# Seven of the twelve column blocks of mod[2] to mod[4]: products on ScalarE and sums on GpSimd, in a diffusion trunk with a mixture of experts

## The chip, the cores and the metric

The kernel runs on one core of a Trainium2 chip. The metric is device time in microseconds (us), the median of several runs. The core's engines are called here by the profile's names: PE (TensorE, matmuls), DVE (VectorE), ACT (ScalarE), POOL (GpSimd), SP (the queue that issues the large transfers).

## The reference

One layer (DEPTH is 1, so mixer 0, the gated convolution, and no context stream). 256 tokens, width 2048, float32, 16 experts.

```python
mod = split(silu(c) @ mod_w + mod_b, 6)                 # six rows of 2048
h   = x * (1 + mod[1]) + mod[0]
gate_b, gate_c, val = split(h @ conv_in_w, 3)           # 2048 -> 3 x 2048
o   = (gate_b * depthwise_conv3(gate_c * val)) @ conv_out_w
x   = layer_norm(ALPHA * x + mod[2] * o)
h2  = x * (1 + mod[4]) + mod[3]
x   = layer_norm(ALPHA * x + mod[5] * hier_moe(h2))     # top-1 group, top-2 of its 4 experts
```

The change concerns mod[2], mod[3] and mod[4]: each is a product of one vector of 2048 with a matrix of 2048 x 2048 from HBM (16 MB each).

## The kernel before

All weights stream through a ring of six SBUF tiles of 128x3072 (`RING`). `get(i)` issues the loads on SP in the order of the list of steps, as far ahead as places in the ring come free; a load waits on its place's last reader.

The product for mod is done in blocks of 512 columns. A block is three ring tiles: 6, 6 and 4 slices of 128x512, one for each of the 16 k tiles `kt`; the vector silu(c) is `sT`, one column for each k tile. A block is made in one of two ways. On TensorE (`gemv_rows` for mod[2] and mod[5], `gemv_cols` for the others): 16 matmuls with `sT` as the stationary operand into a PSUM tile `gv`, line 273 or 300. On VectorE (`gemv_cols` with `on_vector`, chosen by `ON_V`): ScalarE writes the first product into a tile `rows` (line 275), VectorE adds the other 15 (line 278), two at each split (`VN`). For mod[2] the four partial rows of `gv` are added and broadcast to all partitions by a matmul with a selector, `gb` (line 313), and copied into `mod2b` (line 314). For mod[3] and mod[4] the block is transposed, `gc` (line 250), and reduced.

The input projection `conv_in_w` runs in steps (`cin_step`). A step takes a tile with three parts (gate_b, gate_c, val). For each part `split` has ScalarE cast it to a rounded hi (line 395, names `hic`), VectorE subtract for lo (line 396, `loc`), and TensorE run 24 matmuls of 256 columns (lines 403 to 405) with the two halves of h. hi and lo have two buffers each (`whi`, `wlo`). In a full step's names, `hic8_22` is the hi of the step that begins at k tile 8, column group 2, part 2.

The first four column groups are done in five passes over k (`KGS`: 2, 2, 4, 4 and 4 k tiles), called pass 0 to 4 here, since h becomes known block by block from mod[0] and mod[1]; each pass adds into `acc` (line 464). The blocks of mod[0] and mod[1] of the next pass, and so many tiles of mod[2] to mod[4] as `EXTRA` says, are merged among the pass's first three steps. Then come the other four column groups, four steps each, and the output projection `conv_out_w` (`cout_step`, two splits of 1024 columns each, names `hio`), which multiplies by `mod2b` (line 565) and, for its second and third quarter, has GpSimd add the result to x (line 569). The rest of the tiles of mod[2] to mod[4] is merged among these, one for each step. `router_prep` then needs mod[3] and mod[4]. The experts' weights follow, 302 MB.

The program's order on each engine is not the order of the code alone: the scheduler places instructions of one engine by when it expects their operands. What order came out is shown below, with the change.

Of the kernel before, what the change touches and what calls it, by code (L numbers as in the profile page):

```python
# [9 lines left out]
F32 = mybir.dt.float32  # L10
# [9 lines left out]
P = 128  # L20
# [10 lines left out]
ACC_GROUPS = 4  # L31
YB = 4
DRIP = (1, 6, 3)
EXTRA = [0, 1, 0, 0, 12]
KGS = [2, 2, 4, 4, 4]
BEFORE = 4
EARLY = 3
VN = 2
AT = 1
ON_V = [[0, 1, 0, 1], [0, 1, 1, 1]]  # L40
CG = 8

CAPS = [32, 128, 128, 128, 64, 64, 64] + [32] * 9
# [23 lines left out]
def trunk_kernel(  # L67
# [33 lines left out]
    def aux_tile(name):  # L101
        return psum.tile([P, 512], F32, tag="aux", bufs=2, name=name)
# [125 lines left out]
                      start=True, stop=True)  # L228


    pending, queue = [], []

    def mod_load(m, c0, n, t0, nt):
        def load(w):
# [3 lines left out]
            )  # L238
        return load

    def gemv_cols(m, c0, n, on_vector=False):


        box = {}
        nb, k0 = n // P, c0 // P

        def late():
            pt = aux_tile(f"gc{m}_{c0}")
            for i in range(nb):
                TE.transpose(pt[:, i * P : (i + 1) * P], box["r"][:, i * P : (i + 1) * P], ident)  # L250
            sm = const.tile([P, 4], F32, tag="gsum", bufs=2, name=f"gs{m}_{c0}")
            V.tensor_reduce(out=sm[:, :nb], in_=pt[:, :n].rearrange("p (i c) -> p i c", i=nb)[:, :, :: 1 if on_vector else 32],
                            axis=AX.X, op=ALU.add)
            V.scalar_tensor_tensor(
                out=modT[:, m, k0 : k0 + nb], in0=sm[:, :nb], scalar=1.0 if m in (1, 4) else 0.0,
                in1=modbT[:, m * KT + k0 : m * KT + k0 + nb], op0=ALU.add, op1=ALU.add)

        per = min(KT, 3072 // n)
        for t0 in range(0, KT, per):
            nt = min(per, KT - t0)  # L260

            def work(w, t0=t0, nt=nt):
                if t0 == 0:
                    if on_vector:
                        box["r"] = p1.tile([P, 512], F32, tag="rows", bufs=2, name=f"rows{m}{c0}")
                    else:
                        box["ps"] = aux_tile(f"gv{m}_{c0}")
                for k in range(nt):
                    kt = t0 + k
                    g = kt % 4  # L270
                    ws = w[:, k * n : (k + 1) * n]
                    if not on_vector:
                        TE.matmul(box["ps"][32 * g : 32 * g + 32, :n], sT[:, kt : kt + 1].to_broadcast([P, 32]), ws, start=kt < 4, stop=kt >= 12)  # L273
                    elif kt == 0:
                        S.mul(box["r"][:, :n], ws, sT[:, kt : kt + 1])
                    else:
                        def fn(ws=ws, kt=kt):
                            V.scalar_tensor_tensor(out=box["r"][:, :n], in0=ws, scalar=sT[:, kt : kt + 1],  # L278
                                                   in1=box["r"][:, :n], op0=ALU.mult, op1=ALU.add)
                            if kt == KT - 1:  # L280
                                pending.append(late)
                        queue.append(fn)
                if t0 + nt == KT and not on_vector:
                    box["r"] = p1.tile([P, 512], F32, tag="rows", bufs=2, name=f"rows{m}{c0}")
                    S.copy(box["r"][:, :n], box["ps"][:, :n])
                    pending.append(late)

            yield mod_load(m, c0, n, t0, nt), work

    def gemv_rows(m, q, dst, tile_fn, done):  # L290

# [22 lines left out]
        S.copy(dst, ps[:, :])  # L314


    bias_rows = {}
    for m, pool in ((2, p1), (5, const)):
        bias_rows[m] = pool.tile([P, 512], F32, name=f"bias{m}")
        G.memset(bias_rows[m], 0.0)  # L320
        S.dma_start(bias_rows[m][0:128:32, :], mod_b[0, m * D : (m + 1) * D].rearrange("(q c) -> q c", c=512))
# [25 lines left out]
    S.dma_start(rtw[:, :, 0:4], rt_grp_w[0].rearrange("(t p) c -> p t c", p=P))  # L347
    S.dma_start(rtw[:, :, 4:20], rt_exp_w[0].rearrange("(t p) c -> p t c", p=P))

    ii = p1.tile([P, P], I32, tag="rows", bufs=2, name="ii_128")  # L350
    G.iota(ii, pattern=[[1, P]], base=1, channel_multiplier=0)
    iota = const.tile([P, P], F32, name="iota")
    V.tensor_copy(iota, ii)
    ii = p1.tile([P, NOV], I32, tag="rows", bufs=2, name="ii_ov")
    G.iota(ii, pattern=[[1, NOV]], base=1, channel_multiplier=0)
    io32 = const.tile([P, NOV], F32, name="io32")
    V.tensor_copy(io32, ii)
# [34 lines left out]
    def split(src, n, name):  # L392
        hi = p1.tile([P, 1024], F32R, tag="whi", bufs=2, name=f"hi{name}")
        lo = p1.tile([P, 1024], F32R, tag="wlo", bufs=2, name=f"lo{name}")
        S.copy(hi[:, :n], src)  # L395
        V.tensor_sub(lo[:, :n], src, hi[:, :n].bitcast(F32))  # L396
        for fn in queue[:VN]:
            fn()
        del queue[:VN]
        return hi, lo  # L400

    def mm3(ps, whi, wlo, ahi, alo, start, stop):
# [49 lines left out]
        yhi[g], ylo[g] = yh, yl  # L452

    accs = [big_tile(f"acc{g}").rearrange("p (a t) -> p a t", a=3) for g in range(ACC_GROUPS)]
    mod2b = p1.tile([P, D], F32, name="mod2b")
    stats = const.tile([P, 2, 4, 6], F32, name="stats")

    def acc_step(i, g, hook=None):
# [19 lines left out]

    rp = {}

    def router_prep():
        flush()
        V.tensor_mul(G4, T2t[:, 0:16], modT[:, 4, :])
        V.tensor_mul(B3, T2t[:, 32:48], modT[:, 4, :])
        V.tensor_add(B3, B3, modT[:, 3, :])
        t3 = p1.tile([P, KT, 32], F32, tag="rows", bufs=2, name="rtB")
        sums = const.tile([P, 40], F32, name="rsums")
        V.tensor_tensor(out=t3, in0=rtw, in1=B3[:, :, None].to_broadcast([P, KT, 32]), op=ALU.mult)
        V.tensor_reduce(out=sums[:, 0:20], in_=t3[:, :, 0:20].rearrange("p k c -> p c k"), axis=AX.X, op=ALU.add)
        V.tensor_tensor(out=rtw, in0=rtw, in1=G4[:, :, None].to_broadcast([P, KT, 32]), op=ALU.mult)  # L490
        V.tensor_reduce(out=sums[:, 20:40], in_=rtw[:, :, 0:20].rearrange("p k c -> p c k"), axis=AX.X, op=ALU.add)

        def late():
            ps = aux_tile("rsum")
            TE.matmul(ps[:, 0:40], onesF.to_broadcast([P, P]), sums, start=True, stop=True)
            V.tensor_add(rb, rb, ps[:, 0:20])
            V.tensor_copy(rsum, ps[:, 20:40])

            pt = aux_tile("gbT")
            TE.transpose(pt[:KT, 0:P], G4, ident)  # L500
            TE.transpose(pt[:KT, P : 2 * P], B3, ident)
# [13 lines left out]
            V.tensor_copy(GB.rearrange("p s (q j) -> p s q j", j=4), ps[:, 0:32].rearrange("p (s j q) -> p s q j", s=2, j=4))
        pending.append(late)
# [799 lines left out]
```

## Time and profile before

| | us |
|---|---|
| median of 3 runs (1299.0 to 1299.91) | 1299.4 |
| the profiled execution, device time | 1300.78 |
| its span in the trace | 1299.1 |
| mean granted TensorE clock, share of full | 0.958 |

The profile is of one execution. Its page gives each engine's busy time; the trace behind it can be asked for stretches, for the instructions of one engine in time order, and for groups of like instructions. Matmuls are pipelined, so groups of different lines overlap, and a group's busy time is the union of its own spans.

### The profile page before, as it was taken

What the parts mean: (1) busy time and instruction counts of PE and PEld (TensorE: products, weight loads), DVE (VectorE), ACT (ScalarE), POOL (GpSimd) and SP (SyncE); (2) the same over time, 40 slices, a digit from 0 to 9 for tenths busy, and PEclk for the clock granted to TensorE, in tenths of its full rate; (3) what the DMA queues carried; (4) which work ended last, traced back from release to release, by engine and by line L of the source; (5) the groups of instructions that cost most, each with busy time, mean ns of one, the idle gap of its engine ahead of it and who ended that gap; (6) DMA issues with size and microseconds to landing.
All of it is one profiled execution on the core that took longest, in us unless ns stands there. A gap on an engine that the chain in (4) does not pass through costs nothing. (4 is left out here: it accounts for less than half of the span.)

```text
span 1299.1 us, 19675 instructions
## 1 busy us (share of the span) xinstructions
PE 1148.7 (88%) x7871; PEld 755.3 (58%) x7871; DVE 669.4 (52%) x1257; ACT 364.7 (28%) x634; POOL 36.2 (3%) x66
## 2 busy tenths in 40 slices
PE   4999999999999999887789997999689997789982
PEld 2778886878699965543257543674157443444352
DVE  1664555687879978442255642573146431123226
ACT  1332333433344424240035312451026110100020
POOL 1000000000300030000000000000000000000000
PEclk7999999999999999698899999999899999899996
DMA  9999889899999878899998899999999899999991
GB/s 310 372 388 396 301 286 399 305 315 338 348 316 347 306 270 282 366 412 430 429 409 349 321 422 428 405 360 376 428 430 425 338 429 429 429 428 430 429 396 69
DMA packets 151105, 475.61 MB, mean 366 GB/s; under 512 B 11000, under 2 KB 70104, under 8 KB 126688
## 3 DMA queue, kind: packets, MB, share of 16 engines
q1 hardware_dynamic: 145984, 471.89, 92.4%
q10 hardware_dynamic: 5024, 2.40, 0.6%
q8 instruction: 64, 1.05, 0.3%
q14 instruction: 33, 0.27, 0.1%
HBM read 472.16 MB, written 2.10 MB: 365 GB/s over the span
## 5 line engine op out<-in xcount | busy, mean ns | idle before, releaser
L986 PE MATMUL gue<-w,xgp 128*32 128x384 f32 (+1 forms) x1664 | 219.1, 538 | 63.6 <-DMA w<-in_ex_w_up_dram 55.7
L403 PE MATMUL ci<-hhi,hic 128*128 128x256 f32 x768 | 219.6, 287 | 2.3 <-ACT hic L395 1.4
L405 PE MATMUL ci<-hhi,loc 128*128 128x256 f32 x768 | 217.3, 284 | 3.8 <-DVE loc L396 3.6
L404 PE MATMUL ci<-hlo,hic 128*128 128x256 f32 x768 | 216.9, 283 | 0.6 <-DVE hlo L390 0.4
L986 PEld LDWEIGHTS gue<-w,xgp 128*32 128x32 f32 (+1 forms) x1664 | 81.3, 123 | 198.3 <-issue 90.1
L403 PEld LDWEIGHTS ci<-hhi,hic 128*128 128x128 f32 x768 | 145.4, 190 | 14.6 <-issue 8.4
L395 ACT CAST hic<-w 128x1024 fp32r<-128x1024 f32 (+1 forms) x108 | 102.5, 953 | 178.8 <-PE ci L404 153.3
L405 PEld LDWEIGHTS ci<-hhi,loc 128*128 128x128 f32 x768 | 145.1, 189 | 9.4 <-DVE loc L396 6.6
L404 PEld LDWEIGHTS ci<-hlo,hic 128*128 128x128 f32 x768 | 145.5, 189 | 5.4 <-DVE hlo L390 2.3
L396 DVE TENSOR_TENSOR loc<-w,hic 128x1024 fp32r<-128x1024 f32 (+1 forms) x108 | 118.5, 1106 | 34.2 <-ACT hic L395 32.0
L733 DVE TENSOR_TENSOR parts<-w,parts 128x384 fp32r<-128x384 f32 (+1 forms) x168 | 97.8, 612 | 56.8 <-ACT parts L732 55.5
L732 ACT CAST parts<-w 128x384 fp32r<-128x384 f32 (+1 forms) x168 | 89.7, 559 | 79.2 <-PE gue L983 59.5
L1005 ACT COPY gse<-gue 128x384 f32<-128x384 f32 x16 | 7.7, 481 | 313.9 <-PE gue L986 313.9
L858 PEld LDWEIGHTS gap<-ohp,xt 128*128 128x128 f32 x512 | 66.0, 209 | 22.6 <-issue 16.0
L858 PE MATMUL gap<-ohp,xt 128*128 128x128 f32 (+2 forms) x512 | 70.2, 294 | 5.0 <-DVE xgp L826 5.0
L986 PE MATMUL gue<-w,xfp 128*128 128x384 f32 x192 | 71.5, 495 | 1.7 <-DMA w<-in_ex_w_gate_dram 1.7
L273 PE MATMUL gv<-w,sT 128*32 128x512 f32 (+1 forms) x416 | 57.1, 567 | 7.5 <-DMA w<-in_mod_w_dram 7.5
L464 DVE TENSOR_TENSOR acc<-acc,ci 128x512 f32<-128x512 f32 x48 | 32.9, 686 | 58.8 <-PE ci L405 58.6
L1092 DVE TENSOR_TENSOR Y<-dne,m 32x512 f32<-32x512 f32 (+3 forms) x84 | 40.7, 484 | 37.4 <-PE dne L944 34.1
L278 DVE SCALAR_TENSOR_TENSOR rows<-w,sT,rows 128x512 f32<-128x512 f32 x75 | 57.8, 771 | 1.3
L558 PE MATMUL co<-loo,yh 128*128 128x512 f32 x128 | 51.5, 402 | 3.0 <-DVE loo L396 3.0
L826 DVE TENSOR_SCALAR xgp<-gap,GB 128x32 f32<-128x32 f32 (+1 forms) x104 | 31.5, 314 | 43.6 <-ACT xgp L824 43.1
(311 smaller groups left out, 1452.7 us busy)
## 6 DMA issues: line engine op xcount, KB each, us to landing
w<-in_ex_w_gate_dram SPq DMA_DIRECT2D x64, 1536.0 KB, 14.7
w<-in_ex_w_up_dram SPq DMA_DIRECT2D x64, 1536.0 KB, 16.8
w<-in_ex_w_down_dram SPq DMA_DIRECT2D x60, 1536.0 KB, 14.0
w<-in_mod_w_dram SPq DMA_DIRECT2D x48, 1536.0 KB, 8.9
w<-in_conv_in_w_dram SPq DMA_DIRECT2D x84, 512.0 KB, 6.9
w<-in_mod_w_dram SPq DMA_DIRECT2D x22, 1024.0 KB, 8.2
w<-in_conv_out_w_dram SPq DMA_DIRECT2D x16, 1024.0 KB, 6.6
w<-in_conv_in_w_dram SPq DMA_DIRECT2D x24, 256.0 KB, 6.3
```

The costliest lines, as they stand in the source:

```text
L273: TE.matmul(box["ps"][32 * g : 32 * g + 32, :n], sT[:, kt : kt + 1].to_broadcast([P, 32]), ws, start=kt < 4, stop=kt >= 12)
L278: V.scalar_tensor_tensor(out=box["r"][:, :n], in0=ws, scalar=sT[:, kt : kt + 1], in1=box["r"][:, :n], op0=ALU.mult, op1=ALU.add)
L395: S.copy(hi[:, :n], src)
L396: V.tensor_sub(lo[:, :n], src, hi[:, :n].bitcast(F32))
L403: TE.matmul(ps, whi, ahi, start=start, stop=False)
L404: TE.matmul(ps, whi, alo, start=False, stop=False)
L405: TE.matmul(ps, wlo, ahi, start=False, stop=stop)
L558: TE.matmul(pso[h][:, :], yh[:, k, a:b], wl, start=False, stop=False)
L732: S.copy(hi[:, :n], src)
L733: V.tensor_sub(lo[:, :n], src, hi[:, :n].bitcast(F32))
L858: TE.matmul(ps[:, k * n : (k + 1) * n], xn[:, h, (k0 + k) * P : (k0 + k + 1) * P], oh[:, h, :n], start=h == 0, stop=h == 1)
L986: TE.matmul(dst, big[0][:, KF.index(kt), :] if cc == 128 else xg[:, kt, :cc], src, start=st_, stop=sp_)
```

## The change

- mod[2] no longer uses TensorE for its products. `gemv_all` has ScalarE multiply each slice in place in its ring tile (`S.mul(ws, ws, ...)`) and GpSimd add it to the block's columns of `mod2b`, 64 products in all. `mod2b` starts as zeros with the bias in its first partition, so that the sum over partitions, still a matmul and a copy for each block (`finish`, tiles `gb`), includes the bias.
- Of mod[3] and mod[4], three blocks (`SHARED`) are made in the same way into a tile `rows`, the other five by VectorE. None is left to TensorE. Before, five were VectorE's and three TensorE's.
- The products wait in a list `shared`; each split issues one or two of them. `flush_shared` issues what is left ahead of the first step of the output projection, and in `router_prep`.
- `EXTRA` loads four of these tiles in each of passes 2, 3 and 4, in place of one in pass 1 and twelve in pass 4.
- `rows` has three buffers, one more than before; the memset of `mod2b` and the load of its bias stand at the program's start.

```diff
-EXTRA = [0, 1, 0, 0, 12]
+EXTRA = [0, 0, 4, 4, 4]
...
-ON_V = [[0, 1, 0, 1], [0, 1, 1, 1]]
+
+SHARED = [[0, 1, 0, 1], [0, 1, 0, 0]]
...
-    pending, queue = [], []
+    pending, queue, shared = [], [], []
+
+    def add_product(r, ws, kt, then):
+
+        def fn():
+            S.mul(ws, ws, sT[:, kt : kt + 1])
+            G.tensor_tensor(out=r(), in0=r(), in1=ws, op=ALU.add)
+            if kt == KT - 1:
+                then()
+        shared.append(fn)
...
-    def gemv_cols(m, c0, n, on_vector=False):
+    def gemv_cols(m, c0, n, how="PE"):
...
+        def row_tile():
+            box["r"] = p1.tile([P, 512], F32, tag="rows", bufs=3, name=f"rows{m}{c0}")
+
...
                     elif kt == 0:
-                        S.mul(box["r"][:, :n], ws, sT[:, kt : kt + 1])
+                        def fn(ws=ws):
+                            row_tile()
+                            S.mul(box["r"][:, :n], ws, sT[:, 0:1])
+                        (shared if how == "shared" else queue).append(fn)
+                    elif how == "shared":
+                        add_product(lambda: box["r"][:, :n], ws, kt, lambda: pending.append(late))
                     else:
...
+    def gemv_all(m, q, dst):
+
+        def finish():
+            ps = aux_tile(f"gb{m}{q}")
+            TE.matmul(ps[:, :], onesF.to_broadcast([P, P]), dst, start=True, stop=True)
+            S.copy(dst, ps[:, :])
+
+        for t0, nt in ((0, 6), (6, 6), (12, 4)):
+            def work(w, t0=t0, nt=nt):
+                for k in range(nt):
+                    add_product(lambda: dst, w[:, k * 512 : (k + 1) * 512], t0 + k, lambda: pending.append(finish))
+
+            yield mod_load(m, q * 512, 512, t0, nt), work
...
+    mod2b = p1.tile([P, D], F32, name="mod2b")
+    G.memset(mod2b, 0.0)
+    S.dma_start(mod2b[0:1, :], mod_b[0:1, 2 * D : 3 * D])
     bias_rows = {}
-    for m, pool in ((2, p1), (5, const)):
+    for m, pool in ((5, const),):
...
-        for fn in queue[:VN]:
-            fn()
-        del queue[:VN]
+        for todo_, n in ((queue, VN), (shared, 2 if len(shared) > 4 else 1)):
+            for fn in todo_[:n]:
+                fn()
+            del todo_[:n]
         return hi, lo
...
+    def flush_shared():
+        while shared:
+            shared.pop(0)()
+        old = pending[:]
+        pending.clear()
+        for fn in old:
+            fn()
+
     def router_prep():
+        flush_shared()
         flush()
...
         if m == 2:
-            o = mod2b[:, q * 512 : (q + 1) * 512]
-            return list(gemv_rows(m, q, o, aux_tile, lambda: pending.append(lambda: finish_rows(m, q, o))))
-        return list(gemv_cols(m, q * 512, 512, ON_V[m - 3][q]))
+            return list(gemv_all(m, q, mod2b[:, q * 512 : (q + 1) * 512]))
+        return list(gemv_cols(m, q * 512, 512, "shared" if SHARED[m - 3][q] else "DVE"))
...
-            rest += fs[:2] + qt + fs[2:]
+            rest += fs[:2] + ([(None, lambda w: flush_shared())] if g == ACC_GROUPS else []) + qt + fs[2:]
```

The order on the engines moves most in passes 2 and 3. ScalarE, from the cast of pass 3's third step on, before (w39 and w42 are projection tiles, gv0_1536 a block of mod[0]):

```order
L395 CAST hic8_21_1647<-w39_1474 128x1024
L285 COPY rows01536_1593<-gv0_1536_1478 128x512
L395 CAST hic8_22_1675<-w39_1474 128x1024
L395 CAST hic8_30_1727<-w42_1585 128x1024
L395 CAST hic8_31_1755<-w42_1585 128x1024
L285 COPY rows11536_1720<-gv1_1536_1599 128x512
L395 CAST hic8_32_1817<-w42_1585 128x1024
L387 ACTIVATE hhi_183<-xT120_1767,modT_105 128x256 x2
L395 CAST hic12_00_1855<-w43_1595 128x1024
L387 ACTIVATE hhi_183<-xT121_1780,modT_105 128x256 x2
```

Casts follow each other there, with one copy between. The same place now (w45 to w48 are tiles of mod[2], w49 the projection tile of the fourth step):

```order
L427 CAST hic8_22_1730<-w44_1513 128x1024
L419 ACTIVATE hhi_183<-xT121_1843,modT_105 128x256
L237 ACTIVATE w45_1523<-w45_1523,sT_94 128x512 x6
L237 ACTIVATE w46_1635<-w46_1635,sT_94 128x512 x4
L237 ACTIVATE w47_1647<-w47_1647,sT_94 128x512 x3
L310 COPY mod2b_108<-gb21_2035 128x512
L237 ACTIVATE w47_1647<-w47_1647,sT_94 128x512 x3
L237 ACTIVATE w48_1655<-w48_1655,sT_94 128x512 x3
L427 CAST hic8_30_1790<-w49_1663 128x1024
L237 ACTIVATE w48_1655<-w48_1655,sT_94 128x512
L427 CAST hic8_31_1822<-w49_1663 128x1024
```

Nineteen products and a copy of a broadcast now stand between the casts hic8_22 and hic8_30. In pass 2 it is the same with w31 to w34, 6, 6, 4 and 3 products ahead of hic4_30, without a copy among them.

TensorE, where block 1 of mod[2] is broadcast, before (in pass 4, behind six of its products):

```order
L300 MATMUL gv21_1974<-w46_1714,sT_94 32x512 x6
L313 MATMUL gb20_1981<-mod2b_189,selG_79 128x512
L300 MATMUL gv21_1974<-w47_1722,sT_94 32x512 x6
L403 MATMUL ci12_10_1996<-hhi_183,hic12_10_1999 128x256
L404 MATMUL ci12_10_1996<-hlo_184,hic12_10_1999 128x256
L405 MATMUL ci12_10_1996<-hhi_183,loc12_10_2000 128x256
```

It stood between products of the next block. Now, at the end of pass 3's third step:

```order
L436 MATMUL ci8_22_1669<-hhi_183,hic8_22_1730 128x256
L437 MATMUL ci8_22_1669<-hlo_184,hic8_22_1730 128x256
L438 MATMUL ci8_22_1669<-hhi_183,loc8_22_1731 128x256
L309 MATMUL gb21_2035<-mod2b_108,onesF_85 128x512
L436 MATMUL ci8_30_1787<-hhi_183,hic8_30_1790 128x256
L437 MATMUL ci8_30_1787<-hlo_184,hic8_30_1790 128x256
L438 MATMUL ci8_30_1787<-hhi_183,loc8_30_1791 128x256
```

The broadcast moved from the middle of pass 4 to between two steps of pass 3. It reads the sums of w34, w45 and w46. GpSimd had none of them before; its queue now holds there:

```order
L238 TENSOR_TENSOR mod2b_108<-mod2b_108,w45_1523 128x512 x6
L238 TENSOR_TENSOR mod2b_108<-mod2b_108,w46_1635 128x512 x4
L238 TENSOR_TENSOR mod2b_108<-mod2b_108,w47_1647 128x512 x6
L238 TENSOR_TENSOR mod2b_108<-mod2b_108,w48_1655 128x512 x6
```

These 22 sums, in this order, are new. Behind 241 us of the trace, at the second quarter of the output projection (rows31536 is a block of mod[3], xt the residual):

```order
L238 TENSOR_TENSOR rows31536_3268<-rows31536_3268,w77_2938 128x512 x5
L238 TENSOR_TENSOR rows31536_3268<-rows31536_3268,w79_3063 128x512 x5
L610 TENSOR_TENSOR xt_87<-xt_87,t100_3302 128x512
L610 TENSOR_TENSOR xt_87<-xt_87,t101_3305 128x512
L238 TENSOR_TENSOR rows31536_3268<-rows31536_3268,w79_3063 128x512
L238 TENSOR_TENSOR rows31536_3268<-rows31536_3268,w81_3160 128x512 x4
```

Two residual sums stand among the sums of the block.

## Rows read from the trace of the kernel before

**Rows 1.** The page's first part: engine, busy us (share of the span), instructions.
```profile
PE 1148.7 (88%) x7871; PEld 755.3 (58%) x7871; DVE 669.4 (52%) x1257; ACT 364.7 (28%) x634; POOL 36.2 (3%) x66
```

**Rows 2.** Stretches: us, engines' busy us (instructions), TensorE clock, DMA share, GB/s.
```profile
132.00:179.00 47.00, 46.73 (x371) 38.22 (x369) 26.59 (x38) 16.09 (x19) 0.00 (x0) 1.00 0.88 318
179.00:241.00 62.00, 57.56 (x432) 40.79 (x432) 38.72 (x55) 22.27 (x32) 0.00 (x0) 1.00 0.95 349
241.00:447.00 206.00, 202.48 (x1479) 179.80 (x1478) 167.22 (x208) 80.20 (x90) 13.54 (x8) 1.00 0.90 319
...
551.00:1285.00 734.00, 631.82 (x4220) 350.04 (x4212) 289.30 (x653) 171.58 (x389) 3.61 (x2) 0.96 0.95 395
```

**Rows 3.** ScalarE in time order: start, us, line, out<-in, [idle before, releaser].
```profile
119.18 1.05 ACT L395 CAST hic<-w 128x1024 fp32r<-128x1024 f32 x1 [1.76 <-PE ci L404]
122.00 1.05 ACT L395 CAST hic<-w 128x1024 fp32r<-128x1024 f32 x1 [1.77 <-PE ci L404]
...
178.82 1.05 ACT L395 CAST hic<-w 128x1024 fp32r<-128x1024 f32 x1 [0.43 <-PE ci L404]
...
240.53 1.05 ACT L395 CAST hic<-w 128x1024 fp32r<-128x1024 f32 x1 [1.80 <-PE ci L404]
243.38 1.05 ACT L395 CAST hic<-w 128x1024 fp32r<-128x1024 f32 x1 [1.80 <-PE ci L404]
```

**Rows 4.** TensorE groups, 178 to 244 us (two rows), then 244 to 447 us.
```profile
L300 PE MATMUL gv<-w,sT 128*32 128x512 f32 x116 | 15.8, 597 | 0.0
L313 PE MATMUL gb<-mod2b,selG 128*128 128x512 f32 x8 | 4.5, 644 | 2.8 <-DVE mod2b L305 2.8
...
L273 PE MATMUL gv<-w,sT 128*32 128x512 f32 x84 | 13.8, 602 | 0.0
```

**Rows 5.** ScalarE: line 275 (ns min/median/max), line 441 as a group, two in a row.
```profile
L275 ACT ACTIVATE rows<-w,sT x5: 717/727/727, 269.6 to 421.8; 128x512 f32<-128x512 f32 x5
...
L441 ACT ACTIVATE v<-u,T2t 128x256 f32<-128x256 f32 x16 | 7.3, 502 | 6.7 <-DVE u L436 6.7
...
447.84 0.91 ACT L441 ACTIVATE v<-u,T2t 128x256 f32<-128x256 f32 x2
```

**Rows 6.** GpSimd's sums (ns min/median/max), and VectorE's subtractions near one, in time order.
```profile
L569 POOL TENSOR_TENSOR xt<-xt,t x16: 1274/1452/2289, 334.9 to 479.1; 128x512 f32<-128x512 f32 x16
...
354.44 1.22 DVE L396 TENSOR_TENSOR loc<-w,hic 128x1024 fp32r<-128x1024 f32 x1 [3.36 <-ACT hic L395]
...
357.15 1.55 DVE L396 TENSOR_TENSOR loc<-w,hic 128x1024 fp32r<-128x1024 f32 x1 [0.29 <-ACT hic L395]
```

**Rows 7.** DMA issues by form: count, KB each, median us from issue to landing.
```profile
w<-in_conv_in_w_dram SPq DMA_DIRECT2D x84, 512.0 KB, 6.9
```

**Rows 8.** Three stretches of 4 us about an idle, and TensorE's first matmul behind it.
```profile
664.00:668.00 4.00, 2.36 (x10) 1.06 (x6) 3.97 (x19) 0.26 (x1) 0.00 (x0) 1.00 1.00 426
668.00:672.00 4.00, 1.27 (x6) 1.00 (x6) 3.08 (x5) 0.44 (x2) 0.00 (x0) 0.96 1.01 430
672.00:676.00 4.00, 4.00 (x11) 2.70 (x10) 2.06 (x4) 1.41 (x4) 0.00 (x0) 0.61 0.99 421
...
670.73 0.44 PE L984 MATMUL gue<-parts,xhp 128*128 128x384 f32 x1 [4.37 <-DVE parts L733]
```

**Rows 9.** TensorE's first instructions, in time order.
```profile
7.90 0.42 PE L203 MATMUL pt<-ident,T 112*128 112x112 f32 x1 [7.90 <-DMA T<-in_mod_b_dram]
...
9.97 2.79 PE L273 MATMUL gv<-w,sT 128*32 128x256 f32 x24
15.21 0.64 PE L273 MATMUL gv<-w,sT 128*32 128x256 f32 x8 [2.46 <-DMA w<-in_mod_w_dram]
```

More of the change, by code (lines that the diff above doesn't have):

```diff
@@ L251, in late @@
             sm = const.tile([P, 4], F32, tag="gsum", bufs=2, name=f"gs{m}_{c0}")
-            V.tensor_reduce(out=sm[:, :nb], in_=pt[:, :n].rearrange("p (i c) -> p i c", i=nb)[:, :, :: 1 if on_vector else 32],
+            V.tensor_reduce(out=sm[:, :nb], in_=pt[:, :n].rearrange("p (i c) -> p i c", i=nb)[:, :, :: 32 if how == "PE" else 1],
                             axis=AX.X, op=ALU.add)
@@ L262, in work @@
             def work(w, t0=t0, nt=nt):
[L263 to L267, printed above, removed]
+                if t0 == 0 and how == "PE":
+                    box["ps"] = aux_tile(f"gv{m}_{c0}")
                 for k in range(nt):
@@ L271, in work @@
                     ws = w[:, k * n : (k + 1) * n]
-                    if not on_vector:
+                    if how == "PE":
                         TE.matmul(box["ps"][32 * g : 32 * g + 32, :n], sT[:, kt : kt + 1].to_broadcast([P, 32]), ws, start=kt < 4, stop=kt >= 12)
                     elif kt == 0:
-                        S.mul(box["r"][:, :n], ws, sT[:, kt : kt + 1])
+                        def fn(ws=ws):
[4 more added lines that the diff above has]
+                        add_product(lambda: box["r"][:, :n], ws, kt, lambda: pending.append(late))
                     else:
@@ L282, in work @@
                         queue.append(fn)
-                if t0 + nt == KT and not on_vector:
-                    box["r"] = p1.tile([P, 512], F32, tag="rows", bufs=2, name=f"rows{m}{c0}")
+                if t0 + nt == KT and how == "PE":
+                    row_tile()
                     S.copy(box["r"][:, :n], box["ps"][:, :n])
@@ L348, in trunk_kernel @@
     S.dma_start(rtw[:, :, 4:20], rt_exp_w[0].rearrange("(t p) c -> p t c", p=P))
-    ii = p1.tile([P, P], I32, tag="rows", bufs=2, name="ii_128")
+    ii = p1.tile([P, P], I32, tag="rows", bufs=3, name="ii_128")
     G.iota(ii, pattern=[[1, P]], base=1, channel_multiplier=0)
@@ L353, in trunk_kernel @@
     V.tensor_copy(iota, ii)
-    ii = p1.tile([P, NOV], I32, tag="rows", bufs=2, name="ii_ov")
+    ii = p1.tile([P, NOV], I32, tag="rows", bufs=3, name="ii_ov")
     G.iota(ii, pattern=[[1, NOV]], base=1, channel_multiplier=0)
@@ L454, in trunk_kernel @@
     accs = [big_tile(f"acc{g}").rearrange("p (a t) -> p a t", a=3) for g in range(ACC_GROUPS)]
-    mod2b = p1.tile([P, D], F32, name="mod2b")
     stats = const.tile([P, 2, 4, 6], F32, name="stats")
@@ L485, in router_prep @@
         V.tensor_add(B3, B3, modT[:, 3, :])
-        t3 = p1.tile([P, KT, 32], F32, tag="rows", bufs=2, name="rtB")
+        t3 = p1.tile([P, KT, 32], F32, tag="rows", bufs=3, name="rtB")
         sums = const.tile([P, 40], F32, name="rsums")
```

## The prediction

> **What bounds the kernel now.** I read the page's busy times first: TensorE is busy for 88% of the span, VectorE 52%, ScalarE 28%, GpSimd 3% [rows 1]. That average hides two regimes, so I cut the span by stage [rows 2]. From 132 to 447 us TensorE is busy 97% of the time at full clock while the DMA engines are at 88 to 95%: the convolution's projections are bound by TensorE, with transfers not far behind. From 551 to 1285 us the experts' weights move at 395 GB/s, DMA share 0.95: that stage is bound by transfers, and ends as much earlier or later as it starts. So whatever moves the end of the projections moves the end of the kernel by about as much.
>
> Next I read ScalarE's casts in order of time, because they pace the projections. A step of the projection is three splits: ScalarE casts a third of the tile (hi), VectorE subtracts (lo), TensorE runs 24 matmuls. There are two hi buffers, so a cast starts when TensorE has finished the split two before it. Undisturbed casts stand 2.82 us apart (119.18, 122.00) and wait for TensorE [rows 3]: 2.82 us is TensorE's time for a split, and from one split's end it has two splits, 5.6 us, in hand before it needs the cast that this end releases plus one more.
>
> **What the change takes away.** Pass 4 now carries nearly all of mod[2]: its casts go from 178.82 to 240.53, 61.7 us for twelve splits that need 12 x 2.82 = 33.8 [rows 3]. The 27.9 us over are 58 of the 64 products of mod[2] on TensorE, their broadcasts, six products of mod[3], and the waits around them. (TensorE's own rows for the products there are 15.8 us [rows 4]; the rest is order and waits, and goes too.) The four broadcasts stay, 4.5 us in all; one falls into a stall counted below, so 3.4 us stay. The first chunk of mod[2], six products in an earlier pass, is worth 2 to 4 us of TensorE or transfer; I take 3. Behind 241 us the three blocks of mod[3] and mod[4] on TensorE leave: 13.8 us [rows 4]. Together 27.9 - 3.4 + 3 + 13.8 = 41 us of TensorE's path go away. VectorE keeps five blocks, other ones.
>
> **What it adds, and where.** 112 products on ScalarE and 109 sums on GpSimd. A product of 128x512 with a pointer took 0.727 us; two adjacent activations of 0.502 took 0.91, so neighbours overlap by about 0.09, and I take 0.63 in a row, 0.73 as the upper end [rows 5]. A sum of two 128x512 tiles on GpSimd took 1.27 to 2.29 us, median 1.45 [rows 6]. By busy time all this fits: 112 x 0.63 = 71 us for ScalarE, 109 x 1.4 = 153 for GpSimd, over some 300 us. What decides is where the products stand in ScalarE's queue, and the order shows it: not two to a split, as the code's drip reads, but in bunches.
>
> Pass 2: behind the cast hic4_22 stand 19 products, and only then comes hic4_30, which TensorE needs next. From the end of split ci4_20 ScalarE needs 1.05 (cast) + 0.57 (hhi) + 19 x 0.63 + 1.05 = 14.6 us, TensorE has 5.6 us of work: it idles 9 us (11 at 0.73). Queued behind the bunch are all casts of the next step, and the subtractions that wait for them. I take 9.4 with hand-offs.
>
> Pass 3: here the bunch holds a round trip as well. Thirteen products, then the copy of the broadcast gb21, then six more, then the cast hic8_30. The copy waits for TensorE, which waits for GpSimd's ten sums of w45 and w46. From the end of ci8_20: 1.05 + 0.57 + 0.7 + ten sums + 1.1 (broadcast) + 0.6 (copy) + 6 x 0.63 + 1.05 = 8.9 us and ten sums. VectorE has little to do meanwhile, so a sum costs near its shortest, 1.28, and a hand-off, 1.35: 22.4 us, less the 5.6 in hand: TensorE idles 17 us (16 to 26 between the shortest and the longest sum).
>
> Ring tiles: w34 is freed by the 22nd sum of its bunch, some 31 us after the bunch began, and w40, the projection tile of pass 3's second step, takes that place. TensorE reaches it 36 us after the bunch began; the first third of such a tile lands 6.9 us after its issue in the median [rows 7], with other transfers under way, so at 38: 0 to 5 us of wait, I take 2. In pass 4 the products are spread, two or three to a split; casts 12.6, products 12.6, convolution and copies 7 us make 32 of 34 us of ScalarE: 0 to 6, I take 3. Clock: after an idle 4.37 us TensorE was granted 0.61 of its clock in the next 4 us (1.2 GHz for most of them) [rows 8], so about 1.5 us is lost behind each long idle; two of them, 3 us (0 to 8).
>
> Passes: -27.9 + 3.4 - 3 + 9.4 + 17 + 2 + 3 + 3 = +7 us, from -1 to +20.
>
> Behind them, between two casts, stand blocks of 5, 6, 4, 6, 6, 4 and 4 products. Of a block 1.8 us is free (2.82 - 1.05) and some 0.4 is slack, so n x 0.63 - 2.2 is lost: 6 us in all (0 to 9). The transposes gc3_1536 wait for GpSimd's 15 sums of mod[3]'s last block and two residual sums that stand between them, 17 x 1.45 = 25 us from the block's first product, while TensorE comes by after the two splits in hand and four of the output projection, 17 us, and its stalls of 3: a wait of 2 to 10, I take 6. VectorE shares: its subtraction of 1.22 us took 1.55 beside a sum [rows 6], and it is busy 167 of 206 us there [rows 2]. Each of 45 sums costs it 0.3, 14 us if all of it shows; most hides in its free fifth: 5 (0 to 14). Sum: -13.8 + 6 + 6 + 5 = +3 us, from -12 to +19.
>
> The start: the memset of mod2b is four times as wide and stands ahead of the identity, and its row of bias is issued ahead of ScalarE's table load. Both lie under TensorE's wait for T until 7.90 and for weights until 15.21 [rows 9]; 0, up to 2 us if that cover is gone.
>
> **Total.** The profiled execution took 1300.8 us (span 1299.1 and 1.7 around it): 1300.8 + 7 + 3 = 1311. The median of the runs shown is 1.4 us lower, 1299.4: 1310 on its scale. A measurement tells about 0.2%, 2.6 us, from no change.
>
> **One rule against the trace.** VectorE's subtraction of two tiles and GpSimd's sum disturb each other [rows 6]: 1.55 against 1.22 us on the one, 2.29 against 1.27 on the other, as if the sum waited out a subtraction of about 1.0 us. The Trainium skill (SBUF — State Buffer, section "SBUF: two separate sides") says that the pair is an exclusive lock held for the whole instruction, also against a VectorE instruction with two SBUF inputs, and that the loser fully blocks. The trace agrees in the longest sums. By that rule VectorE's own products would wait for the sums too; what that would cost by the rows is the third rival below.
>
> **The rivals.**
> 1. *The relief wins* (faster). Speaks for it: 41 us are really removed and both idles rest on static order. If sums run at 1.28 with no hand-off, products at 0.63, w40 comes in time, the clock holds, and the waits behind 241 us hide: -41 + 9 + 16 + 3 = -13, so 1286. If the queue's bunches found ScalarE so early that nothing showed, 1259; but the cast ahead of each bunch needs a buffer that TensorE frees, so I give that next to nothing. Chance 0.25 for faster.
> 2. *Even.* Costs and relief meet within 2.6 us: 1297 to 1302. Chance 0.08.
> 3. *GpSimd and VectorE block each other* (much slower). Behind 241 us VectorE runs a subtraction and two products of two SBUF tiles per split, 2.7 of 2.82 us. If each of 45 sums makes VectorE wait 1.28 us, that is 58 us against 39 free (206 - 167 [rows 2]): 19 in place of 5, and the sums, at 2.29 between such instructions, hold gc3_1536 and ring tiles longer, some 4 more. 1310 + 18 = 1328. It decides from about 0.9 us a sum. Against it: beside today's 16 sums the spread casts show far less. Chance 0.20.
> 4. *The ring starves the loads.* If GpSimd runs at 1.7 (13.54 us for eight sums [rows 2]), w34 is freed 37 us after the bunch begins: the load lands 6 us later than above, and what is queued behind it on SP's queue, the next six tiles, with it: 1310 + 10 = 1320. Chance 0.12.
> 5. *The forecast*: two idles of about 9 and 17 us and small stalls eat the relief: 1303 to 1318. Chance 0.35.
>
> **How the numbers follow.** Faster 0.25, same 0.08, slower 0.12 + 0.20 + 0.35 = 0.67. The bounds of the two sums are -13 and +39; not all ends meet, so the range reaches from the first rival's 1286 to the third's 1328, with about 0.1 left out on each side; the forecast alone has 1303 to 1318.
>
> **What would show it.** Right: TensorE idle about 9 us ahead of hic4_30 and 17 ahead of hic8_30, ScalarE dense in both, GpSimd dense in the second; pass 4 near 39 us in place of 61.7; products in neighbours near 0.63; expert loads starting some 10 us later than now. Wrong: casts of passes 2 and 3 at 2.82 us throughout, or the end of pass 4 earlier than 243 us; then rival 1. A subtraction's mean well above 1.5 us behind 241 us is rival 3; SP waiting long for GpSimd in pass 3, and TensorE for the transfer of ci8_10's tile, is rival 4.

## The result: 64 us slower, not 10

The changed kernel took 1363.9 us (median of 4 runs, 1359.5 to 1365.5) against 1299.7 before, measured beside it: a ratio of 1.049, 95% interval 1.046 to 1.052. The sign was forecast; the size was not, and the time lies far above the range. The profiled execution took 1362.9 us, its span is 1361.1: 62.0 more than before. The page's first part, as [rows 1]:

```profile
PE 1137.6 (84%) x7647; PEld 766.3 (56%) x7647; DVE 704.9 (52%) x1253; ACT 427.2 (31%) x739; POOL 207.4 (15%) x175
```

TensorE does 11 us less, and the kernel is 62 longer. The stretches, as [rows 2]: the first two are passes 2 and 3, the third pass 4, the fourth holds most of the output projection's first quarter and all of its second, the last is the experts' part; the three lines behind are shorter pieces for the clock.

```profile
86.00:135.00 49.00, 38.28 (x315) 31.36 (x314) 25.10 (x40) 25.38 (x38) 10.14 (x8) 0.97 1.03 377
135.00:220.00 85.00, 60.90 (x419) 50.35 (x420) 35.94 (x40) 34.84 (x49) 52.29 (x36) 0.82 0.80 288
220.00:270.00 50.00, 40.57 (x297) 38.13 (x295) 45.46 (x44) 29.02 (x42) 34.43 (x22) 0.90 0.71 249
...
300.00:420.00 120.00, 91.04 (x519) 77.72 (x519) 91.26 (x96) 51.21 (x65) 61.42 (x38) 0.89 0.78 270
...
612.00:1345.00 733.00, 632.02 (x4216) 351.40 (x4208) 288.75 (x649) 171.55 (x388) 3.62 (x2) 0.96 0.95 396
...
200.00:208.00 8.00, 2.08 (x2) 0.50 (x2) 0.00 (x0) 2.25 (x4) 7.61 (x7) 0.50 1.03 369
208.00:216.00 8.00, 4.12 (x17) 3.82 (x18) 3.86 (x2) 5.75 (x9) 7.67 (x5) 0.50 0.63 209
...
384.00:392.00 8.00, 1.38 (x6) 1.29 (x7) 0.32 (x2) 0.00 (x0) 7.69 (x7) 0.52 0.72 248
```

The experts' part is as long as before (733 against 734 us, 396 GB/s): as argued, it only starts later, and all of the loss lies ahead of it. There TensorE, at clock 1.00 before [rows 2], is busy 61 of 85, 41 of 50 and 91 of 120 us, and the clock it is granted in these stretches is 0.82, 0.90 and 0.89. What TensorE waited for, first before (86 to 551 us), then after (86 to 612, the same work); total, times, longest:

```profile
PE co L558 <- DVE loo L396: 3.0, 4, 1.6
PE gb L313 <- DVE mod2b L305: 2.8, 2, 1.4
...
PE ci L405 <- DVE loc L396: 2.4, 5, 0.8
```

```profile
PE ci L438 <- DVE loc L428: 20.3, 14, 4.6
PE ci L436 <- ACT hic L427: 20.1, 7, 8.5
PE co L599 <- DVE loo L428: 14.7, 6, 5.0
PE gb L309 <- POOL mod2b L238: 10.3, 1, 10.3
PE gc L260 <- POOL rows L238: 9.9, 1, 9.9
```

The second, fourth and fifth line are the waits that the forecast named: ScalarE's bunches, the broadcast gb21, the transposes gc3_1536. The first and third, 35 us for VectorE's lo, are not; before they were 5.4. VectorE's groups show why. In the output projection's first quarter, before (241 to 330 us), then the part of it in which GpSimd's sums run after (296 to 330), with two rows in time order:

```profile
L396 DVE TENSOR_TENSOR loo<-w,hio 128x1024 fp32r<-128x1024 f32 x10 | 12.2, 1220 | 7.0 <-ACT hio L395 7.0
L565 DVE TENSOR_TENSOR t<-co,mod2b 128x512 f32<-128x512 f32 x8 | 5.3, 684 | 0.0
L567 DVE SCALAR_TENSOR_TENSOR xt<-xt,t 128x512 f32<-128x512 f32 x8 | 5.2, 683 | 0.0
```

```profile
L428 DVE TENSOR_TENSOR loo<-w,hio 128x1024 fp32r<-128x1024 f32 x6 | 11.5, 1930 | 0.0
L608 DVE SCALAR_TENSOR_TENSOR xt<-xt,t 128x512 f32<-128x512 f32 x6 | 6.4, 1098 | 0.0
L606 DVE TENSOR_TENSOR t<-co,mod2b 128x512 f32<-128x512 f32 x8 | 5.2, 683 | 2.3 <-PE co L600 2.3
...
301.32 3.48 DVE L293 SCALAR_TENSOR_TENSOR rows<-w,sT,rows 128x512 f32<-128x512 f32 x2
304.72 2.29 DVE L428 TENSOR_TENSOR loo<-w,hio 128x1024 fp32r<-128x1024 f32 x1
```

The subtraction rose from 1.22 to 1.93 us and the update of xt from 0.68 to 1.10, while t, whose first operand co lies in PSUM, stayed at 0.68. Here only instructions with both tensors in SBUF suffer, while GpSimd's sums run.

### The profile page after: what moved, and what is told of

It is laid out like the page before. It is cut to its first block, busy times and chain, and to the rows that moved or that the text cites. A ratio compares the mean times of both kernels' runs of the same rounds, so it can differ in the third digit from the quotient of the medians.

```text
span 1361.1 us, 19548 instructions
## 1 busy us (share of the span) xinstructions
PE 1137.6 (84%) x7647; PEld 766.3 (56%) x7647; DVE 704.9 (52%) x1253; ACT 427.2 (31%) x739; POOL 207.4 (15%) x175
## 5 line engine op out<-in xcount | busy, mean ns | idle before, releaser
L436 PE MATMUL ci<-hhi,hic 128*128 128x256 f32 x768 | 223.4, 291 | 20.7 <-ACT hic L427 20.1
L438 PE MATMUL ci<-hhi,loc 128*128 128x256 f32 x768 | 223.3, 292 | 20.6 <-DVE loc L428 20.3
L437 PE MATMUL ci<-hlo,hic 128*128 128x256 f32 x768 | 221.3, 288 | 1.4 <-DVE hlo L422 1.3
L428 DVE TENSOR_TENSOR loc<-w,hic 128x1024 fp32r<-128x1024 f32 (+1 forms) x108 | 130.5, 1213 | 76.4 <-ACT hic L427 74.8
L436 PEld LDWEIGHTS ci<-hhi,hic 128*128 128x128 f32 x768 | 151.0, 197 | 28.9 <-ACT hic L427 24.4
L438 PEld LDWEIGHTS ci<-hhi,loc 128*128 128x128 f32 x768 | 150.2, 196 | 28.2 <-DVE loc L428 27.1
L437 PEld LDWEIGHTS ci<-hlo,hic 128*128 128x128 f32 x768 | 150.6, 196 | 3.6 <-DVE hlo L422 2.8
L238 POOL TENSOR_TENSOR mod2b<-mod2b,w 128x512 f32<-128x512 f32 x64 | 96.9, 1515 | 165.2 <-ACT w L237 153.7
L238 POOL TENSOR_TENSOR rows<-rows,w 128x512 f32<-128x512 f32 x45 | 73.8, 1640 | 90.1 <-ACT w L237 86.3
L237 ACT ACTIVATE w<-w,sT 128x512 f32<-128x512 f32 x109 | 70.1, 712 | 0.0
L599 PE MATMUL co<-loo,yh 128*128 128x512 f32 x128 | 55.2, 431 | 15.0 <-DVE loo L428 14.7
## 6 DMA issues: line engine op xcount, KB each, us to landing
w<-in_ex_w_gate_dram SPq DMA_DIRECT2D x64, 1536.0 KB, 14.7
w<-in_ex_w_down_dram SPq DMA_DIRECT2D x60, 1536.0 KB, 13.8
```

Source lines behind the costliest of these rows:

```text
L237: S.mul(ws, ws, sT[:, kt : kt + 1])
L238: G.tensor_tensor(out=r(), in0=r(), in1=ws, op=ALU.add)
L436: TE.matmul(ps, whi, ahi, start=start, stop=False)
L437: TE.matmul(ps, whi, alo, start=False, stop=False)
L438: TE.matmul(ps, wlo, ahi, start=False, stop=stop)
```

## Experiments

The theory after this reading: GpSimd's sums are the cost, through their conflict with VectorE (P) and as links of chains that TensorE waits for; ScalarE's bunches and the clock are the smaller rest. Rivals: the bunches themselves; any second engine in the chain; the clock. Ratios are to the kernel before on the same chip.

**e1: without the sums.**

```diff
-            G.tensor_tensor(out=r(), in0=r(), in1=ws, op=ALU.add)
+            r()
```

> The changed kernel without GpSimd's 109 sums (that part of the computation is left out: mod[2] holds only its bias, three blocks of mod[3] and mod[4] only their first product). ScalarE's 109 products, their bunches, the loads and the broadcasts stay. Theory S (the sums are the cost: they hold gb21, gc3_1536 and ring tiles and slow VectorE): of TensorE's 85 us idle between 86 and 612 us only the two bunches of products stay, about 8.5 in pass 2 and 9 in pass 3, beside some 15 that the kernel before has too; 1299.7 - 35 (work taken from TensorE) + 18 (bunches) + 8 (clock) = about 1291, from 1283 to 1305. Theory B (ScalarE's bunches are the cost): little changes, above 1335.

Measured: 1306.9 us, 1.005 (1.002 to 1.009). The sums, by their conflict with VectorE and by what waits for them, are worth 57 of the 64 us. What stays of TensorE's waits:

```profile
PE ci L436 <- ACT hic L427: 17.3, 4, 8.5
PE co L599 <- DVE loo L428: 9.6, 6, 3.6
```

The bunches' two waits (8.5 and 7.1) are there as expected, and theory B, above 1335, is out. But the time is 2 us above theory S's bound. The first casts of pass 4 and behind it show where:

```profile
205.81 1.05 ACT L427 CAST hic<-w 128x1024 fp32r<-128x1024 f32 x1 [1.85 <-PE ci L437]
...
240.99 1.04 ACT L427 CAST hic<-w 128x1024 fp32r<-128x1024 f32 x1
```

Pass 4 takes 35.2 us in place of 61.7 [rows 3], so its relief comes in full once the sums are gone, and its end is only 0.5 us late. The relief of three blocks behind it does not show: by the projection's last casts the kernel is 6 us late. There TensorE waits 9.6 us for VectorE's loo, and its mean granted clock is 0.97 from 241 to 504 us, where it was 1.00 before.

**e2: 45 sums alone, on the kernel before.** They add a tile to itself that nobody reads any more.

```diff
+            G.tensor_tensor(out=bias_rows[2], in0=bias_rows[2], in1=bias_rows[2], op=ALU.add)
```

> The kernel before with 45 sums of 128x512 added on GpSimd into a tile that nobody reads any more; they can start when mod[2] is done, at about 241 us, and run one behind the other. No product, ring tile or wait hangs on them. Theory P (GpSimd's sum and VectorE's instructions of two SBUF operands keep each other out): 45 x about 1.05 us of VectorE against some 20% of free time in 75 us; VectorE's lo comes late, TensorE idles 15 to 30 us and its clock falls: 1315 to 1335; the subtraction of 1.22 reads about 2.28 beside a sum. Rival (VectorE is slowed only by the 0.33 us that the trace of before showed): at most 1305.

Measured: 1322.9 us, 1.017 (1.010 to 1.024): 22 us for sums that nothing waits for. VectorE, 241 to 330 us:

```profile
L397 DVE TENSOR_TENSOR loc<-w,hic 128x1024 fp32r<-128x1024 f32 x13 | 19.5, 1498 | 8.1 <-ACT hic L396 8.1
L397 DVE TENSOR_TENSOR loo<-w,hio 128x1024 fp32r<-128x1024 f32 x8 | 15.0, 1880 | 5.7 <-ACT hio L396 5.7
...
L569 DVE TENSOR_TENSOR t<-co,mod2b 128x512 f32<-128x512 f32 x8 | 5.3, 680 | 1.0 <-PE co L563 1.0
```

The means come near those of the changed kernel, and t is again untouched; the 2.28 us that was expected beside a sum is the longest (2.30), not the mean. VectorE's busy time rose from 669.4 to 693.1 us, 0.53 a sum, and TensorE's waits for lo from 5.4 to 20.1. P holds, with e7 below as its control.

**e3 and e4: each half alone.** In e3 mod[3] and mod[4] are as before, in e4 mod[2] and the spread of the loads.

```diff
-        return list(gemv_cols(m, q * 512, 512, "shared" if SHARED[m - 3][q] else "DVE"))
+        return list(gemv_cols(m, q * 512, 512, "DVE" if ON_V[m - 3][q] else "PE"))
```

> Only mod[2] as in the changed kernel; mod[3] and mod[4] as before (five blocks on VectorE, three on TensorE), loads spread as in the change. If the costs of the two halves add up: passes as in the changed kernel, +31 us at the end of pass 4, and the rest as before: about 1330 (1322 to 1337). If the loss in the rest came from the passes (late tiles, a cold clock): above 1345.

> Only mod[3] and mod[4] as in the changed kernel (three blocks on ScalarE and GpSimd, five on VectorE); mod[2] and the spread of the loads as before. If the costs add up: passes as before, and the rest as in the changed kernel, +29: about 1329 (1318 to 1336). If the rest's loss was brought on by the passes: near 1300.

Measured: 1335.8 us, 1.027 (1.020 to 1.034), and 1324.1 us, 1.018 (1.011 to 1.025). 35 + 24 = 59 of the 64, each with an interval of 9 us to either side from two runs: within that the halves add up, and the loss of the rest was not brought on by the passes.

**e5: the same tiles, spread over the steps.** The bunch stands where four mod[2] tiles are loaded ahead of the fourth step's tile; here they are merged between the blocks of mod[0] and mod[1].

```diff
-        nxt += late[sum(EXTRA[:i]) : sum(EXTRA[: i + 1])]
+        add = late[sum(EXTRA[:i]) : sum(EXTRA[: i + 1])]
+        nxt = merge(add, nxt) if nxt and add else nxt + add
```

> The changed kernel with one thing moved: in passes 2 to 4 its four tiles are merged between the blocks of mod[0] and mod[1], so that one stands in each of the first three steps, not all four behind the third. ScalarE's 19 products in a row become groups of at most 6 or 7. If the waits of passes 2 and 3 come from the bunch (8.5 ahead of hic4_30, 10.3 and 5.3 about gb21, 3.5 for the late ring tile, and some 6 us of clock behind them), most of these 33 us go: 1330 to 1345. If they come from the pace of GpSimd's sums whatever their place (64 x 1.5 us, ring tiles held, VectorE blocked), little goes: above 1350.

Measured: 1340.1 us, 1.031 (1.026 to 1.035): 24 us better than the change.

```profile
PE ci L438 <- DVE loc L428: 21.8, 15, 5.1
PE co L599 <- DVE loo L428: 11.0, 5, 4.5
...
PE ci L436 <- ACT hic L427: 6.8, 5, 2.1
```

Waits for ScalarE fell from 20.1 to 6.8 and the one for gb21 is gone; those for lo are 32.8 where they were 35.0.

**e6 and e7: the sums on VectorE; GpSimd busy without reading.** e7 puts 135 memsets where e2 had its 45 sums.

```diff
-            G.tensor_tensor(out=r(), in0=r(), in1=ws, op=ALU.add)
+            V.tensor_tensor(out=r(), in0=r(), in1=ws, op=ALU.add)
```

> The changed kernel with the 109 sums on VectorE instead of GpSimd (about 0.69 us each, 75 us more for VectorE, 31 of them behind 241 us where it had 39 free); ScalarE's products, bunches and loads as in the change. If GpSimd's pace and its conflict with VectorE cost most: VectorE is through with a block in half the time, nothing blocks; the bunches stay (17 us of waits): 1305 to 1330. If what costs is that a second engine has to read the products at all (round trip, ring tiles held): above 1345.

> Control for the spare sums: the kernel before with 135 memsets of the same 128x512 tile on GpSimd in the same place, 0.53 us each, 71 us in all, as long as the 45 spare sums took (65.8). They read nothing. Theory P (two engines that both read two operands from SBUF keep each other out): no effect, 1297 to 1304, the subtraction stays at 1.22. Rival (any work of GpSimd at that time, by its SBUF writes or its queue, slows VectorE): 1315 or more, as with the sums.

Measured: e6 1319.2 us, 1.015 (1.010 to 1.019), 45 better than the change, although VectorE now makes the 109 sums itself (busy 734 us; 705 in the changed kernel). e7 1302.2 us, 1.001 (0.999 to 1.003), no difference, with 71 us of memsets:

```profile
L404 POOL MEMSET bias<- 128x512 f32 x135 | 71.2, 527 | 238.0 <-DVE mod2b L306 230.3
...
L397 DVE TENSOR_TENSOR loc<-w,hic 128x1024 fp32r<-128x1024 f32 x18 | 22.0, 1222 | 12.3 <-ACT hic L396 12.3
```

So it is not GpSimd's work as such, nor its writes, but its sums, which read two SBUF tiles, beside VectorE's instructions that read two. A GpSimd instruction that reads only one was not tried.

**e9: spare matmuls in two waits.** On e1, so that only the bunches make the waits.

```diff
+                if g == 3 and a == 0 and k0 in (4, 8):
+                    for _ in range(68 if k0 == 4 else 56):
+                        TE.matmul(pss[0][:, :T], hhi[:, 0, :P], hhi[:, 0, :], start=True, stop=True)
```

> The kernel of e1 (the changed kernel without GpSimd's sums, that part is left out) with 68 and 56 spare matmuls of 256 columns ahead of the first matmul of ci4_30 and of ci8_30, where TensorE waited 8.5 and 7.1 us for ScalarE's bunches. They write into the step's own PSUM tile before its first real matmul clears it, and take 8 and 6.6 us at 0.118 each: inside the two waits. Theory C (a wait costs more than its length, since TensorE comes back at half its clock): the granted clock behind both waits stays 1.00 and the time falls 3 us for each, from e1's 1.0053 of the kernel before to 1.000 (1300 to 1302). Rival (what the clock loses there is made up by the slack of the next wait): no change, 1306 to 1308.

Measured: 1307.9 us, 1.005 (1.003 to 1.007), as e1. Behind the first wait, e1's and then e9's stretch:

```profile
136.00:144.00 8.00, 7.38 (x42) 7.08 (x43) 4.06 (x4) 3.95 (x6) 0.00 (x0) 0.66 1.05 406
```

```profile
136.00:144.00 8.00, 7.00 (x56) 6.79 (x57) 5.05 (x5) 4.90 (x7) 0.00 (x0) 1.00 1.05 406
```

The clock stays full and 56 matmuls in place of 42 are done; the third cast behind the wait comes at 140.30 instead of 141.99, 1.7 us earlier, not 3, since the first two still wait for ScalarE. The second half failed as an experiment: copies of the broadcasts in ScalarE's queue now waited for the spare matmuls, and the 1.7 us were lost again there. So theory C's 3 us a wait fell; what a wait's cold clock costs at the kernel's end stays open, between nothing and some 2 us.

**e8, e10 and e12: the relief without GpSimd.** In e8 VectorE makes two of mod[2]'s four blocks in passes 2 and 3, product and sum in one instruction; e10 also drops the memset and the load at the start (the last two lines of the edit); e12 is e10 with all four blocks and the change's own `EXTRA`. In all three mod[3] and mod[4] are as before, and the tiles are spread as in e5.

```diff
-            S.mul(ws, ws, sT[:, kt : kt + 1])
-            G.tensor_tensor(out=r(), in0=r(), in1=ws, op=ALU.add)
+            V.scalar_tensor_tensor(out=r(), in0=ws, scalar=sT[:, kt : kt + 1], in1=r(), op0=ALU.mult, op1=ALU.add)
...
-EXTRA = [0, 0, 4, 4, 4]
+EXTRA = [0, 0, 3, 3, 7]
...
-    G.memset(mod2b, 0.0)
-    S.dma_start(mod2b[0:1, :], mod_b[0:1, 2 * D : 3 * D])
```

> A version meant to keep the relief without its costs: two of mod[2]'s four blocks are made by VectorE alone (product and sum in one instruction of about 0.75 us) in passes 2 and 3, where it is busy 55%, spread over the steps; the other two stay on TensorE in pass 4; mod[3] and mod[4] as before. Nothing on GpSimd or ScalarE. Half of pass 4's 27.9 us over goes, about 14, less one or two broadcasts: 1288 (1280 to 1297). Rival (VectorE's 16 products a pass make its lo late, or the loads moved forward come too late): 1300 or more.

> The kernel of e8 without the memset of mod2b and the load of its bias at the start: the first product of a block is written by ScalarE, and VectorE adds the bias row to it. In e8 the casts of the first pass stood 3.5 us later than before. If the start's two instructions cost that: 1293.5 (1290 to 1296). If the 3.5 us come from the loads' new order: as e8, 1297.

> As e10, but all four blocks of mod[2] on VectorE (22 products a pass instead of 16 in passes 2 and 3, and the rest in pass 4), none on TensorE. TensorE is relieved of 16 us; VectorE has 27 + 17 of 47 us in passes 2 and 3. If VectorE keeps up: 1288 (1284 to 1294). If its lo comes late, or the four tiles a pass hold the projection's tiles back: 1297 or more.

Measured: e8 1297.0 us, 0.997 (0.995 to 0.999), less gain than expected; e10 1287.8 us, 0.990 (0.988 to 0.993), better than both kernels and than expected; e12 1311.8 us, 1.007 (1.004 to 1.010), the rival. e10, passes 2 and 3, and the first cast behind pass 4:

```profile
86.00:133.00 47.00, 43.77 (x347) 35.76 (x348) 37.57 (x58) 15.67 (x20) 0.00 (x0) 1.00 1.06 400
133.00:178.00 45.00, 43.21 (x355) 36.10 (x354) 34.23 (x49) 15.17 (x19) 0.00 (x0) 1.00 1.06 398
...
231.05 1.05 ACT L430 CAST hic<-w 128x1024 fp32r<-128x1024 f32 x1 [1.77 <-PE ci L440]
```

That cast stood at 240.53 [rows 3]: 9.5 us gained, and kept. In both passes the DMA engines are now busy throughout (share 1.06) at 398 to 400 GB/s, where pass 3 had moved 318 [rows 2]. With six more products a pass in e12, VectorE's lo comes late: 14.7 us of TensorE's waits, 4.2 in e10, and the granted clock in the same two stretches is 0.93 and 0.92. That goes the way of the rival; that it makes up all of the 24 us between e10 and e12 was not shown.

**e11: both repairs.** e5's spread and e6's sums on VectorE together.

> The changed kernel with both repairs: tiles spread over the steps as in e5 (24 us better than the change) and sums on VectorE as in e6 (45 better). If bunches and GpSimd are two separate costs: 1364 - 24 - 45 = 1295 (1290 to 1302). If both repairs remove the same waits: 1315 to 1320, no better than e6.

Measured: 1307.6 us, 1.006 (1.004 to 1.008). 56 us of 24 + 45 come back: the two causes are separate for the most part, with some 13 us in common. Neither number of the expectation held.

## Where the prediction was right and where not

The sum can be closed for the stretch from 86 us to the experts' part, 465 us before and 526 after. TensorE's idle time there rose from 14.6 to 85.0, by 70.4; its busy time fell by 9.4; 70.4 - 9.4 = 61 of the 62 us.

| term | forecast | measured | from |
|---|---|---|---|
| work taken from TensorE | -41, waits among the work included | -33, without waits | its groups of products, 71.6 to 37.8, broadcasts +0.7 |
| bunch of pass 2 | 9.4 | 8.5 | idle ahead of hic4_30 |
| bunch and round trip of pass 3 | 17 | 15.6 | 10.29 + 5.29 |
| late ring tile w40 | 2 | 3.5 | idle ahead of ci8_10 |
| pass 4 | 3 | 9.8 | three waits for lo |
| blocks of products behind 241 us | 6 | 2.8 | the other waits for ScalarE |
| gc3_1536 | 6 | 9.9 | idle ahead of it |
| VectorE's share behind 241 us | 5 | about 20 | waits for lo, 35.0 - 9.8 - 5.4 of before |
| clock | 3 | about 22 | what is left of TensorE's busy time: -33 + 2 of the start + 22 = -9 |
| start | 0 | 2.1 | first cast of pass 2 |

**Right:** where and why TensorE would stand still in passes 2 and 3. ScalarE's rows in pass 2, then those of pass 3:

```profile
122.04 1.05 ACT L427 CAST hic<-w 128x1024 fp32r<-128x1024 f32 x1 [1.49 <-issue]
...
123.46 11.74 ACT L237 ACTIVATE w<-w,sT 128x512 f32<-128x512 f32 x19
135.10 1.03 ACT L427 CAST hic<-w 128x1024 fp32r<-128x1024 f32 x1
...
189.03 8.07 ACT L237 ACTIVATE w<-w,sT 128x512 f32<-128x512 f32 x13
205.75 0.59 ACT L310 COPY mod2b<-gb 128x512 f32<-128x512 f32 x1 [8.65 <-PE gb L309]
206.24 3.78 ACT L237 ACTIVATE w<-w,sT 128x512 f32<-128x512 f32 x6
209.92 1.03 ACT L427 CAST hic<-w 128x1024 fp32r<-128x1024 f32 x1
```

19 products in 11.74 us are 0.62 each, as taken from [rows 5]; the copy of the broadcast stands in the middle of pass 3's bunch and waits 8.65 us. TensorE's rows of the same places, and of gc3_1536:

```profile
136.19 0.58 PE L436 MATMUL ci<-hhi,hic 128*128 128x256 f32 x1 [8.48 <-ACT hic L427]
...
203.64 2.08 PE L309 MATMUL gb<-mod2b,onesF 128*128 128x512 f32 x2 [10.29 <-POOL mod2b L238]
211.00 0.58 PE L436 MATMUL ci<-hhi,hic 128*128 128x256 f32 x1 [5.29 <-ACT hic L427]
...
390.62 1.11 PE L260 MATMUL gc<-ident,rows 128*128 128x128 f32 x4 [9.88 <-POOL rows L238]
```

Static order times durations of single rows gave these waits to within 1.5 us; gc3_1536 lies at the end of its bounds, 2 to 10. Of the signs named, products in neighbours near 0.63 came true; pass 4 took 49.9 us, not 39, and the experts' loads start some 61 us later, not 10.

**Wrong, first: the conflict of VectorE and GpSimd.** The step that failed is "Each of 45 sums costs it 0.3 ... most hides in its free fifth: 5 (0 to 14)". Neither half held. The 0.3 came from one subtraction that met a sum for part of its length [rows 6]; in the changed kernel the 35 that lie mostly beside sums took 1.73 us in the mean and up to 2.31, and e2 shows 0.53 us of VectorE for each of 45 sums, less than the 1.28 of rival 3. And little of it hid. The free 39 us were counted over 206 us, but sums that come in rows do not spread over it: e2's 45 stand nearly all between 241 and 303 us, where VectorE, busy 47.3 us before, had 14.7 free. The 23.7 us that they cost VectorE made the kernel 22 us longer.

The price could have been read before the change. The prediction held against rival 3 that today's 16 sums show far less, but its rows show one pair of them [rows 6]. Beside two pairs some 20 us earlier in the same trace:

```profile
334.93 3.53 POOL L569 TENSOR_TENSOR xt<-xt,t 128x512 f32<-128x512 f32 x2 [330.99 <-DVE t L565]
341.61 2.98 POOL L569 TENSOR_TENSOR xt<-xt,t 128x512 f32<-128x512 f32 x2 [3.15 <-DVE t L565]
...
335.37 1.94 DVE L396 TENSOR_TENSOR loo<-w,hio 128x1024 fp32r<-128x1024 f32 x1
...
343.37 3.44 DVE L396 TENSOR_TENSOR loo<-w,hio 128x1024 fp32r<-128x1024 f32 x2
```

One subtraction took 1.94 us, and of the next two, 3.44 us together, one took 2.30: nearly as long as any in the changed kernel. In the mean the six subtractions (loo) that lie mostly beside the 16 sums took 1.65.

The prediction also charged the conflict behind 241 us only, and took pass 4's 3 us from ScalarE's load; the three waits there were all for lo. e7 shows that the conflict needs more of GpSimd than being busy and writing: its sums read SBUF.

The rule that the prediction cites from the Trainium skill (SBUF — State Buffer, section "SBUF: two separate sides"), a lock held for the whole instruction, agrees with the longest of these rows, a rise of 1.09 us beside sums of 1.27 and more; the same section limits it to GpSimd instructions that read SBUF, and e7's unchanged 1.222 us agrees with that as well.

**Wrong, second: the clock.** I priced it for two waits, and there were eleven of 2.3 us and more that the kernel before does not have; TensorE's granted clock fell to half, 1.2 GHz, in and behind several of them (0.50 from 200 to 216 us, 0.52 from 384 to 392). The 22 us are a remainder, and the granted clock bears it out: weighing TensorE's busy time by it in stretches of 2 us gives 33 us lost below full clock in the changed kernel and 12 before, 21 more. e9 says that not all of it would come back with a full clock, since behind such a wait another engine sets the pace as well.

**Wrong, third: the relief behind 241 us.** The 27.9 us over in pass 4 were rightly counted as going, waits and all: in e1 pass 4 is 26.5 us shorter than before. But the 13.8 us behind 241 did not show even without any sum (e1): VectorE's loo was late and the clock lower. That five blocks stay on VectorE does not mean that they stay in places where it has time; that their new places are what made loo late is argued, since the two orders were not compared.

The range had a slip as well: the passes' upper end, +20, is not the sum of its terms' upper ends, -27.9 + 3.4 - 2 + 11 + 26 + 5 + 6 + 8 = 29.5. Even that would not have reached 1364.

**Rival 4,** the starved ring: SP did wait for GpSimd's sums, but TensorE waited 3.5 us for a late tile; a loss, and a small one. **The start,** 0 in the sum: 2.1 us, by the first cast of pass 2, before and after:

```profile
84.63 1.05 ACT L395 CAST hic<-w 128x1024 fp32r<-128x1024 f32 x1 [0.77 <-PE ci L404]
```

```profile
86.77 1.05 ACT L427 CAST hic<-w 128x1024 fp32r<-128x1024 f32 x1
```

In e8 that cast stood at 87.78 and in e10, without the two instructions, at 83.80. Which of the two it was, was not separated.

## What to carry to other kernels

Work given to GpSimd is not free because GpSimd idles: if it reads two SBUF tiles, it delays VectorE's instructions that read two, here by half a microsecond a sum in the mean and by one at the longest, and where VectorE feeds TensorE, the delay stands in TensorE's waits. VectorE's free time hides it only if that time lies where the sums run. One partial overlap is no price for it: look at every meeting in the trace of before, or add a handful of spare instructions to the kernel before, which price it in one run (e2, with e7 as its control). And the place of the loads decides where a scheduler bunches the work that hangs on them: spreading four tiles a pass took back 24 us without moving any work to another engine.

## What the runs showed of the hardware

- Beside GpSimd's sums of two SBUF tiles, VectorE's subtraction took 1.73 us in the mean (1.22 alone) and 2.31 at the longest, and two of its products 3.48 (0.75 for one alone). An instruction with one operand in PSUM kept its 0.68. Beside 71 us of memsets on GpSimd the subtraction kept its 1.22 (e7).
- With TensorE kept at work through an 8.5 us wait the granted clock behind it stayed at 1.00, in place of 0.66.
